# Operands of an RWKV-7 scan prepared in another order: two blocks of items instead of pairs for feature tiles 4 to 7

## The chip, the cores and the metric

The kernel runs on one core of a Trainium2 chip. The metric is device time in microseconds (us) of one execution. TensorE (PE) does the matrix products, VectorE (DVE), ScalarE (ACT) and GpSimd (POOL) the elementwise work, SyncE (SP) issues nearly all transfers between HBM and SBUF, in program order.

## The reference, cut to what matters

The model is a block of depth 2 with a model width of 1024, 512 latent tokens and 256 context tokens. Layer 0 mixes tokens by a bidirectional RWKV-7 recurrence, layer 1 by a Hyena convolution; each mixer stands between two half-step SwiGLU layers. The change lies in layer 0, between its projections and its scan:

```python
k = xk @ w_rkv[1]
w_pre = w0 + einsum(tanh(einsum(xw, w1)), w2)
decay = exp(-exp(-softplus(-w_pre) - 0.5))
a = sigmoid(a0 + einsum(einsum(xa, a1), a2))
kk = heads(k * k_k);  kk = kk / norm(kk)
k_dir = heads(k)[None] * (1 + (ah - 1) * heads(k_a))
ka = kk[None] * ah
S, y = _wkv_scan(S0, _fb(heads(decay)), _fb(k_dir), _both(vh), _both(kk), _fb(ka), _both(rh))
...
y = y + sum(rh * k_bonus * r_k) * vh
g = sigmoid(xg @ g1) @ g2
```

The scan runs over all 768 tokens in both directions (d = 0 and 1). Only latent tokens have outputs, so `r` is needed for the 512 latent tokens alone.

## The kernel before

All activations lie with features on the 128 partitions: eight feature tiles m = 0..7, tokens along the free axis. Each fp32 product is a sum of three products of high and low parts (`hh`, `hl`, `lo`; PE lines L481 to L483).

**Projections.** `rwkv_proj` computes the tokens' projections one after the other: k, r, v and, last, the gate's first factor g1, whose results are called `ev` and stored to the scratch tensors `S_h0` and `S_h1` (DMA line L950). All its products run on PE without a pause where their operands are there.

**Preparation.** `rwkv_prep` is a generator that `rwkv_proj` steps between its products. It turns k, r and two low-rank factors into the operands of the scan. Its unit of work is an item: one feature tile m and one half of the tokens, W = 384 columns. Half 0 is tokens 0 to 383, all latent (`wl` = 384). Half 1 is tokens 384 to 767, of which 128 are latent (`wl` = 128). An item passes through three stages, and at each step the `back` of item i-2, the `middle` of item i-1 and the `front` of item i are interleaved:

- `front`: loads k and r (SP), normalizes (PE L993, DVE L995), and for each direction makes decay and a from two low-rank products (PE L1006 with the high part `l2h`, L1007 with the low part `l2l`; ACT L1009).
- `middle`: for each direction DVE L1029 to L1054, ACT L1030 to L1039, and the product of r with the key, L1049 (outputs `rb` and `r`), on POOL, but on DVE for the last two items (`NVEC` = 2, L1025). It writes the operands `AR` to `S_A[g, d, half]` (L1058) and `KD` to `S_K[g, d, half]` (L1063, L1065), where g is 0 for m < 4 and 1 for m >= 4.
- `back`: one small product (PE L1075), a copy (ACT L1078) and the store to `S_b` (SP L1079).

`lora2(m)` brings the second low-rank factor of tile m: a DMA of 256 KB into `l2r`, an ACT cast into `l2h` (L975), a POOL subtraction into `l2l` (L976). All three have a single buffer, so the next tile's factor can be split only when the last product of the item before has read the old one.

**Scan.** `rwkv_scan` walks blocks of two 64-token chunks for each direction; for each block and g, `load` zeroes half of a tile `AG` (ACT L1140 in the first four pairs) and loads the rest from `S_A` (SP L1143) and `KK` from `S_K` (L1147). The first four blocks read only half 1; the first reader of half 0 is the ninth pair. Then come the scores (PE L1211), copies of them (ACT L1219, L1187), triangular selection (POOL L1188), `lanes` (ACT L1235) and the block's inversion on DVE, which begins with the transpose L1240. From the third pair on, a small POOL memset (L1136) of `AG` stands ahead of its load. `selg` (POOL L1566) multiplies two constants for the scan's output; it waits for four small loads `ysum` (SP L1565).

The order of the first stretch of the scan on PE, DVE and POOL is written out by hand; in the preparation, and on ACT and SP everywhere, a list scheduler orders the instructions when the program is built, so a change in one place can swap neighbours elsewhere.

Of the kernel before, what the change touches and what calls it, by code (L numbers as in the profile page):

```python
# [20 lines left out]
DT = D // P  # L21
# [5 lines left out]
NP = 4  # L27
# [249 lines left out]
class K:  # L277
# [678 lines left out]
    def rwkv_prep(self, bp):  # L956
# [5 lines left out]
        l2 = {}  # L962

        def ps(w):
            return self.psq.tile([P, 512], F32, tag="pq", name=self.nm("pq"))[:, :w]

        def T(tag, w=W, bufs=2):
            return bp.tile([P, W], F32, tag=tag, name=self.nm(tag), bufs=bufs)[:, :w]

        def lora2(m):  # L970
            raw = bp.tile([P, 4, P], F32, tag="l2r", name=self.nm("l2r"), bufs=1)
            hi = bp.tile([P, 4, P], F32R, tag="l2h", name=self.nm("l2h"), bufs=1)
            lo = bp.tile([P, 4, P], F32R, tag="l2l", name=self.nm("l2l"), bufs=1)
            nc.sync.dma_start(raw, self.A["wa2"][m])
            nc.scalar.copy(hi, raw)  # L975
            nc.gpsimd.tensor_tensor(lo, raw, hi.bitcast(F32), ALU.subtract)  # L976
            l2[m] = (hi, lo)

        lora2(0)

        def front(s):
            m, half = s["m"], s["half"]
            mc = slice(m, m + 1)
            o = s["o"] = half * W
            wl = s["wl"] = min(TL - o, W)
            s["nl"] = wl // 64
            k, r = T("k"), T("r", wl)
            nc.sync.dma_start(k, self.S_k[m][:, o : o + W])
            nc.sync.dma_start(r, self.S_r[m][:, o : o + wl])
            hi, lo = l2[m]  # L990
            yield
            pb = ps(W)
            nc.tensor.matmul(pb, self.selT[:, m * P : (m + 1) * P], self.kinv[:, o : o + W], start=True, stop=True)  # L993
            kk = s["kk"] = T("kk")
            nc.vector.scalar_tensor_tensor(kk, k, self.hkk[:, mc], pb, ALU.mult, ALU.mult)  # L995
            s["k"], s["r"] = k, r
            yield
            s["q"], s["a"] = [], []
            for d in range(2):
                q = bp.tile([P, nch, 65], F32, tag=f"q{d}", name=self.nm("q"))  # L1000
                a = T(f"a{d}")
                nc.gpsimd.memset(q[:, :, 0:1], 0.0)
                rows = slice(d * 64, d * 64 + 64)
                for j, (x, t) in enumerate(((self.midw, q[:, :, 1:]), (self.mida, a))):
                    pt = ps(W)
                    nc.tensor.matmul(pt, hi[:, 2 * j + d], x[d][:, o : o + W], start=True, stop=False)  # L1006
                    nc.tensor.matmul(pt, lo[rows, 2 * j + d], x[d][rows, o : o + W], start=False, stop=True)  # L1007
                    b = (self.hw0, self.ha0)[j][:, d, mc]
                    nc.scalar.activation(t, c3(pt) if j == 0 else pt, AF.Tanh, bias=b, scale=0.5)  # L1009
                nc.vector.tensor_scalar(q[:, :, 1:], q[:, :, 1:], 1.0, None, ALU.add)  # L1010
                s["q"].append(q)
                s["a"].append(a)
                if d == 1 and half == 0 and m < DT - 1:
                    lora2(m + 1)
                yield

        def middle(s):
# [50 lines left out]
        def back(s):  # L1068
            m, wl, o = s["m"], s["wl"], s["o"]
            pt = ps(wl)  # L1070
            rks = bp.tile([P, P], F32, tag="rks", name=self.nm("rks"), bufs=1)
            nc.scalar.activation(rks, self.c("bo64"), AF.Copy, scale=self.rk32[:, m : m + 1])
            yield
            for d in range(2):
                nc.tensor.matmul(pt, rks, s["b"][d], start=d == 0, stop=d == 1)  # L1075
            yield
            v = s["b"][0]
            nc.scalar.copy(v, pt)  # L1078
            nc.sync.dma_start(self.S_b[s["m"]][:, o : o + wl], v)  # L1079
            yield  # L1080

        items = [dict(i=2 * m + 1 - half, m=m, half=half) for m in range(DT) for half in (1, 0)]
        n = len(items)
        for i in range(n + 2):
            gens = []
            if 0 <= i - 2:
                gens.append(back(items[i - 2]))
            if 0 <= i - 1 < n:
                gens.append(middle(items[i - 1]))
            if i < n:  # L1090
                gens.append(front(items[i]))
            while gens:
                gens = [x for x in gens if next(x, 0) is None]
                yield
# [1030 lines left out]
```

## Time and profile before

| | us |
|---|---|
| median of 3 runs | 3029.62 |
| lowest to highest | 3029.31 to 3033.85 |
| the profiled execution, its own time | 3036.99 |
| its span from first to last instruction | 3035.0 |

| engine | busy us in the span | share |
|---|---|---|
| PE | 2782.4 | 92% |
| DVE | 1818.3 | 60% |
| ACT | 1163.4 | 38% |
| POOL | 477.7 | 16% |

PE bounds the program as a whole. The change lies in the stretch from about 900 to 1010 us after the span's start and touches what follows it, where the shares differ from these, so the rows below are of that stretch. The mean granted clock of PE over the span is 0.947.

### The profile page before, as it was taken

The page shows a single profiled execution, that of the slowest core. Times are in us where ns is not written, and L with a number is a line of the kernel's source. Part 1 is how long each engine was busy: PE and PEld are TensorE (multiplying, and loading weights), DVE is VectorE, ACT ScalarE, POOL GpSimd, SP SyncE. Part 2 cuts the span into 40 slices and gives each one's busy share as a digit, 9 for nine tenths or more (in the row PEclk, how much of TensorE's full clock was granted, in tenths as well). Part 3 has the DMA queues.
Part 4 walks back from the last instruction along what each step waited for, and adds up shares of the span by engine and source line. Part 5 has one row for each costly group of instructions (what it writes and reads, how often), then busy time and mean ns, then how long its engine had stood idle before and what let it go on. Part 6 is the DMA issues. An engine that isn't in the chain of part 4 may idle for free.

```text
span 3035.0 us, 46673 instructions
## 1 busy us (share of the span) xinstructions
PE 2782.4 (92%) x18394; PEld 2324.9 (77%) x18394; DVE 1818.3 (60%) x3403; ACT 1163.4 (38%) x2007; POOL 477.7 (16%) x647
## 2 busy tenths in 40 slices
PE   8899999978889378887899999999999989899998
PEld 4788888857666366765788889888887777888888
DVE  4656444474798688997655546455365588653334
ACT  3221121255666678874232223322334322332222
POOL 0000000032343445532100000000000054100000
PEclk9999999979989678998899999999999999999999
DMA  5434333313688744434345543455333544232331
GB/s 206 155 106 148 132 128 109 100 37 102 171 211 209 192 117 130 125 86 125 128 146 167 171 162 112 140 183 180 106 116 135 206 143 147 105 124 85 97 106 48
DMA packets 363971, 409.36 MB, mean 135 GB/s; under 512 B 77719, under 2 KB 303127, under 8 KB 362024
## 3 DMA queue, kind: packets, MB, share of 16 engines
q1 hardware_dynamic: 363752, 406.39, 42.4%
q8 instruction: 144, 2.36, 0.3%
q14 instruction: 75, 0.61, 0.1%
HBM read 340.20 MB, written 65.34 MB: 134 GB/s over the span
## 4 chain that ended last, share of the span: by engine, by line
PE 74%; DVE 13%; DMA 4%; ACT 3%; issue 3%; POOL 2%; SPq 0%; DVEq 0%; POOLq 0%; ACTq 0%
PE ps L481 21%; PE ps L482 21%; PE ps L483 21%; DVE Dl L1278 1%; PE sc L1211 1%; DVE wlo L487 1%; DVE Tm L1271 1%; DMA mraw<-in_mod_wt 1%; DVE SV L1350 1%; DVE zt L1946 1%; POOL za L1947 1%; DVE zl L487 1%; PE pf L1759 1%; DMA AG<-S_A 1%; DMA x<-in_xT 1%
## 5 line engine op out<-in xcount | busy, mean ns | idle before, releaser
L482 PE MATMUL ps<-hl,whi 128*128 128x512 f32 (+1 forms) x2064 | 742.4, 362 | 3.5 <-DVE hl L268 3.5
L481 PE MATMUL ps<-hh,whi 128*128 128x512 f32 (+1 forms) x2064 | 732.2, 363 | 14.2 <-ACT hh L267 10.7
L483 PE MATMUL ps<-hh,wlo 128*128 128x512 f32 (+1 forms) x2064 | 735.6, 362 | 2.0 <-DVE wlo L487 2.0
L487 DVE TENSOR_TENSOR wlo<-raw,whi 128x1024 fp32r<-128x1024 f32 (+1 forms) x325 | 392.9, 1215 | 383.6 <-ACT whi L486 382.6
L486 ACT CAST whi<-raw 128x1024 fp32r<-128x1024 f32 (+1 forms) x338 | 344.6, 1028 | 707.8 <-PE ps L482 631.2
L481 PEld LDWEIGHTS ps<-hh,whi 128*128 128x128 f32 x2064 | 386.7, 190 | 78.3 <-ACT hh L267 13.2
L482 PEld LDWEIGHTS ps<-hl,whi 128*128 128x128 f32 x2064 | 392.8, 190 | 64.4 <-DVE hl L268 4.9
L483 PEld LDWEIGHTS ps<-hh,wlo 128*128 128x128 f32 x2064 | 391.8, 190 | 63.4 <-DVE wlo L487 2.9
L481 PE MATMUL ps<-dh,whi 128*128 128x512 f32 (+1 forms) x1072 | 354.3, 336 | 7.8 <-DVE x L660 7.8
L482 PE MATMUL ps<-dl,whi 128*128 128x512 f32 (+1 forms) x1072 | 358.3, 335 | 0.0
L483 PE MATMUL ps<-dh,wlo 128*128 128x512 f32 (+1 forms) x1072 | 357.8, 335 | 0.0
L421 DVE CUSTOM_DVE_ANT_0 mraw<-mraw,mc 128x1024 f32<-128x1024 f32 x128 | 156.5, 1223 | 142.8 <-DMA mraw<-in_mod_wt 141.6
L481 PEld LDWEIGHTS ps<-dh,whi 128*128 128x128 f32 x1072 | 203.5, 190 | 29.4 <-DVE x L660 8.0
L482 PEld LDWEIGHTS ps<-dl,whi 128*128 128x128 f32 x1072 | 204.2, 190 | 20.5
L483 PEld LDWEIGHTS ps<-dh,wlo 128*128 128x128 f32 x1072 | 204.0, 190 | 20.2
L375 POOL COPY mraw<-dl 128x1 f32<-128x1 f32 x128 | 44.8, 364 | 896.3 <-DVE dl L487 631.2
L611 DVE TENSOR_TENSOR sg<-sg,ps 128x512 f32<-128x512 f32 (+1 forms) x110 | 69.1, 633 | 175.6 <-PE ps L483 165.5
L610 ACT ACTIVATE sg<-ps 128x512 f32<-128x512 f32 (+1 forms) x110 | 59.8, 553 | 209.7 <-PE ps L483 202.8
L486 ACT CAST dh<-sg 128x512 fp32r<-128x512 f32 (+1 forms) x110 | 62.1, 575 | 201.2 <-DVE sg L611 201.1
L482 PE MATMUL ps<-xl,whi 128*128 128x512 f32 (+2 forms) x336 | 125.8, 376 | 9.6 <-DVE xl L811 7.1
L481 PE MATMUL ps<-xh,whi 128*128 128x512 f32 (+2 forms) x336 | 123.6, 380 | 9.5 <-issue 5.9
L483 PE MATMUL ps<-xh,wlo 128*128 128x512 f32 (+2 forms) x336 | 123.2, 372 | 0.0
(315 smaller groups left out, 4498.6 us busy)
## 6 DMA issues: line engine op xcount, KB each, us to landing
raw<-in_wgu SPq DMA_DIRECT2D x88, 1024.0 KB, 5.0
mraw<-in_mod_wt SPq DMA_DIRECT2D x128, 512.0 KB, 5.3
raw<-in_wd SPq DMA_DIRECT2D x24, 1024.0 KB, 5.0
raw<-in_wrkv SPq DMA_DIRECT2D x12, 1024.0 KB, 5.9
S_A<-AR SPq DMA_DIRECT2D x32, 384.0 KB, 3.6
AG<-S_A SPq DMA_DIRECT2D x48, 256.0 KB, 4.2
KK<-S_K SPq DMA_DIRECT2D x24, 512.0 KB, 4.5
KL<-S_K SPq DMA_DIRECT2D x48, 256.0 KB, 2.9
```

The source lines that it names most:

```text
L375: self.nc.gpsimd.tensor_copy(raw[:, :1], held)
L421: nc.vector.tensor_tensor_reduce(dst, raw, self.rows[w], 1.0, 0.0, ALU.mult, ALU.add, accum_out=cols[w][:, m : m + 1])
L481: nc.tensor.matmul(out, wh, xh, start=start, stop=False)
L482: nc.tensor.matmul(out, wh, xl, start=False, stop=False)
L483: nc.tensor.matmul(out, wl, xh, start=False, stop=stop)
L486: self.nc.scalar.copy(hi, src)
L487: (self.nc.gpsimd if pool else self.nc.vector).tensor_tensor(lo, src, hi.bitcast(F32), ALU.subtract)
L610: nc.scalar.activation(sg, pg, AF.Silu)
L611: nc.vector.tensor_mul(sg, sg, pu)
L1211: nc.tensor.matmul(sc[:, p_, :, :ns, :], KK[:, c, p_].rearrange("p s t -> p (s t)"), AG[:, c, :, p_, :ns, :], start=True, stop=True,)
L1271: nc.vector.tensor_tensor(tm[:, js, rs], L[:, p, rs].unsqueeze(1).to_broadcast([P, n, w]), Dl[:, js, p : p + 1].to_broadcast([P, n, w]), A ...
L1278: nc.vector.tensor_tensor(Dl[:, js, rs], Dl[:, js, rs], tm[:, js, rs], ALU.subtract)
```

## The change

The sixteen items stay, their work is the same, and tiles 0 to 3 keep their order (half 1, then half 0 of each). For tiles 4 to 7 the order was 4/1, 4/0, 5/1, 5/0, 6/1, 6/0, 7/1, 7/0 (tile/half); it is now 4/1, 5/1, 6/1, 7/1, 4/0, 5/0, 6/0, 7/0. So the tile differs between neighbours in all of these items, and `lora2` is called whenever the next item has another tile: 12 calls in all instead of 8. The last two items, whose L1049 products run on DVE, are now both of half 0 (384 wide); before, they were one of each half.

```diff
-            l2[m] = (hi, lo)
-
-        lora2(0)
+            l2["next"] = (hi, lo)
...
-            hi, lo = l2[m]
+            hi, lo = l2.pop("next")
...
-                if d == 1 and half == 0 and m < DT - 1:
-                    lora2(m + 1)
+                if d == 1 and s["i"] < n - 1:
+                    if items[s["i"] + 1]["m"] != m:
+                        lora2(items[s["i"] + 1]["m"])
+                    else:
+                        l2["next"] = (hi, lo)
...
-        items = [dict(i=2 * m + 1 - half, m=m, half=half) for m in range(DT) for half in (1, 0)]
+
+        order = [(m, half) for m in range(NP) for half in (1, 0)] + [(m, half) for half in (1, 0) for m in range(NP, DT)]
+        items = [dict(i=i, m=m, half=half) for i, (m, half) in enumerate(order)]
         n = len(items)
+        lora2(0)
```

The line numbers of the changed kernel differ by -2 to +4 from those named above (L1211 is L1215 there, L1143 is L1147, L1566 is L1570, L1075 is L1076).

Where instructions stand, three places. The first is SP's queue where the preparation ends and the scan's first loads begin. `S_h` are the stores of the gate's first factor, `AG` and `KK` the scan's loads. Before:

```order
362 L950 DMA S_h1_4898<-ev_1348_8230 32x512
363 L1058 DMA S_A111_4908<-AR_1345_8193 128x6x128
364 L1065 DMA S_K111_4916<-KD_1346_8197 64x6x64
365 L1063 DMA S_K111_4916<-KD_1346_8197 64x6x128
366 L1065 DMA S_K111_4916<-KD_1346_8197 64x6x64
367 L1143 DMA AG_1362_8322<-S_A001_4902 64x2x512
368 L1058 DMA S_A100_4905<-AR_1353_8250 128x6x128
369 L1065 DMA S_K100_4913<-KD_1355_8255 64x6x64
370 L1143 DMA AG_1362_8322<-S_A001_4902 64x2x512
371 L1147 DMA KK_1363_8323<-S_K001_4910 128x2x512
```

And now, from the same store of `S_h1` on:

```order
368 L950 DMA S_h1_4898<-ev_1360_8254 32x512
369 L1566 DMA selg_8341<-in_selq 128x256
370 L1569 DMA ysum_8340<-in_lng 32x256
371 L1066 DMA S_K100_4913<-KD_1367_8279 64x6x64
372 L1569 DMA ysum_8340<-in_lng 32x256
373 L1059 DMA S_A100_4905<-AR_1365_8274 128x6x128
374 L1064 DMA S_K100_4913<-KD_1367_8279 64x6x128
375 L1066 DMA S_K100_4913<-KD_1367_8279 64x6x64
376 L1147 DMA AG_1374_8346<-S_A001_4902 64x2x512 x2
377 L1151 DMA KK_1375_8347<-S_K001_4910 128x2x512
382 L1569 DMA ysum_8340<-in_lng 32x256
386 L1569 DMA ysum_8340<-in_lng 32x256
```

Seven transfers stand between the store of `S_h1` and the first load of the scan, where four stood; the four small loads for `selg`, which stood ahead of the `S_h` stores, are spread out, the last one ten places behind the first `AG` load.

The second place is POOL at the same point of the program, before (`AG_1370` is the second block's first tile):

```order
194 L487 TENSOR_TENSOR xl_1290_7984<-xm_1288_7980,xh_1289_7983 128x512
195 L1566 TENSOR_TENSOR selg_8317<-selg_8317,ysum_8316 128x256
196 L1188 AFFINE_SELECT AG_1362_8322<-AG_1362_8322 64x4x64 x4
197 L1188 AFFINE_SELECT AG_1364_8329<-AG_1364_8329 64x4x64 x2
198 L1136 MEMSET AG_1370_8372 128x4
```

and now (`AG_1382` is the second block's first tile):

```order
195 L976 TENSOR_TENSOR l2l_1325_8088<-l2r_1323_8086,l2h_1324_8087 128x512
196 L487 TENSOR_TENSOR xl_1299_8004<-xm_1297_8000,xh_1298_8003 128x512
197 L1050 TENSOR_TENSOR rb_1313_8053<-r_1252_7823,a0_1259_7845 128x384
198 L1050 TENSOR_TENSOR r_1252_7823<-r_1252_7823,a1_1264_7864 128x384
199 L1192 AFFINE_SELECT AG_1374_8346<-AG_1374_8346 64x4x64 x4
200 L1192 AFFINE_SELECT AG_1376_8353<-AG_1376_8353 64x4x64
201 L1570 TENSOR_TENSOR selg_8341<-selg_8341,ysum_8340 128x256
202 L1192 AFFINE_SELECT AG_1376_8353<-AG_1376_8353 64x4x64
203 L1140 MEMSET AG_1382_8396 128x4
```

`selg` went from ahead of the selections to between them, ahead of the memset of the second block's tile; and a split of the low-rank factor (`l2l`) now stands ahead of the last `xl` of the projections.

The third place is PE from the end of the projections to the scan's first scores, before:

```order
4449 L482 MATMUL ps_1347_8205<-xl_1290_7984,whi_1328_8112 32x512
4450 L483 MATMUL ps_1347_8205<-xh_1289_7983,wlo_1329_8113 32x512
4451 L1075 MATMUL pq_1349_8234<-rb_1333_8150,rks_1350_8235 128x128
4452 L1075 MATMUL pq_1349_8234<-r_1299_8014,rks_1350_8235 128x128
4453 L1211 MATMUL ps_1367_8339<-AG_1362_8322,KK_1363_8323 128x128 x4
4454 L1211 MATMUL ps_1368_8350<-AG_1362_8322,KK_1363_8323 128x128 x4
4455 L1075 MATMUL pq_1360_8282<-rb_1354_8253,rks_1361_8283 128x384
```

and now:

```order
4437 L482 MATMUL ps_1359_8229<-xl_1299_8004,whi_1340_8138 32x512
4438 L483 MATMUL ps_1359_8229<-xh_1298_8003,wlo_1341_8139 32x512
4439 L1076 MATMUL pq_1330_8112<-rb_1313_8053,rks_1331_8113 128x384
4440 L991 MATMUL pq_1336_8130<-kinv_807_5887,selT_4942 128x384
4441 L1004 MATMUL pq_1348_8181<-mw0_4938,l2h_1324_8087 128x384
4450 L1076 MATMUL pq_1361_8258<-rb_1345_8176,rks_1362_8259 128x384
4451 L1076 MATMUL pq_1361_8258<-r_1308_8034,rks_1362_8259 128x384
4452 L1215 MATMUL ps_1379_8363<-AG_1374_8346,KK_1375_8347 128x128 x4
4455 L1215 MATMUL ps_1384_8404<-AG_1376_8353,KK_1377_8354 128x128 x4
4456 L1076 MATMUL pq_1372_8306<-rb_1366_8277,rks_1373_8307 128x384
```

The last item's low-rank products moved from ahead of the last projection products to behind them, and the last item's two `back` products from between the first scores to behind all four groups of the first block.

## Rows read from the trace of the kernel before

**Rows 1.** Busy time by stretch: PE, PEld, DVE, ACT, POOL; granted clock; DMA share; GB/s.

```profile
900.00:940.00 40.00, 38.50 (x183) 28.82 (x182) 34.84 (x53) 27.92 (x61) 14.67 (x16) 0.96 0.96 243
980.00:990.00 10.00, 6.91 (x19) 3.33 (x18) 10.00 (x21) 7.04 (x14) 1.73 (x3) 0.83 0.74 169
990.00:1000.00 10.00, 0.79 (x2) 0.50 (x2) 5.69 (x13) 7.27 (x12) 3.49 (x1) 0.53 0.96 243
...
1060.00:1380.00 320.00, 265.08 (x4539) 219.75 (x4538) 280.77 (x849) 244.78 (x539) 144.19 (x228) 0.88 0.40 112
```

**Rows 2.** Timeline of PE: start, us, line, out<-in, [idle before <-releaser].

```profile
986.08 0.39 PE L483 MATMUL ps<-xh,wlo 128*32 128x512 f32 x1
...
1004.08 3.76 PE L1211 MATMUL ps<-AG,KK 128*128 128x128 f32 x16 [11.73 <-DMA AG<-S_A]
1007.63 0.88 PE L1075 MATMUL pq<-rb,rks 128*128 128x384 f32 x2
...
1008.99 1.05 PE L1211 MATMUL sc<-AG,KK 128*128 128x128 f32 x8
```

**Rows 3.** Timeline of SP's transfers: time of issue, time the issue took, line.

```profile
989.92 0.63 SPq L950 DMA_DIRECT2D S_h<-ev  x1
...
994.03 0.60 SPq L1143 DMA_DIRECT2D AG<-S_A  x1
...
996.93 0.61 SPq L1147 DMA_DIRECT2D KK<-S_K  x1
...
1009.69 0.33 SPq L1079 DMA_DIRECT2D S_b<-rb  x1
...
1012.07 1.25 SPq L1143 DMA_DIRECT2D AG<-S_A  x2
```

**Rows 4.** Timeline of ACT at the start of the scan.

```profile
993.58 3.20 ACT L1140 ACTIVATE AG<-ones 64x1024 f32<-64x1024 f32 x3 [2.09 <-POOL selg L1566]
...
1009.19 0.48 ACT L1078 COPY rb<-pq 128x384 f32<-128x384 f32 x1
...
1011.37 0.62 ACT L486 CAST gh<-gr 128x512 fp32r<-128x512 f32 x1
...
1013.33 2.13 ACT L1140 ACTIVATE AG<-ones 64x1024 f32<-64x1024 f32 x2
1015.37 2.48 ACT L1235 COPY Dl<-Bc 32x512 f32<-32x512 f32 x4
```

**Rows 5.** Timeline of DVE, end of the preparation and first two inversions.

```profile
965.71 1.45 DVE L1010 TENSOR_SCALAR q<-q 128x384 f32<-128x384 f32 x1
...
973.25 0.34 DVE L1010 TENSOR_SCALAR q<-q 128x384 f32<-128x384 f32 x1
...
986.95 0.28 DVE L1049 TENSOR_TENSOR rb<-r,a 128x128 f32<-128x128 f32 x1
...
1004.91 0.56 DVE L1049 TENSOR_TENSOR rb<-r,a 128x384 f32<-128x384 f32 x1 [2.57 <-DMA S_b<-rb]
...
1017.94 1.93 DVE L1240 STREAM_TRANSPOSE L<-Dl 128x1024 f32<-128x1024 f32 x1 [11.81 <-ACT Dl L1235]
...
1034.90 1.91 DVE L1240 STREAM_TRANSPOSE L<-Dl 128x1024 f32<-128x1024 f32 x1 [0.24 <-ACT Dl L1235]
```

**Rows 6.** POOL's group of the factor splits, 780 to 1005 us: busy us, mean ns.

```profile
L976 POOL TENSOR_TENSOR l2l<-l2r,l2h 128x512 fp32r<-128x512 f32 x7 | 11.8, 1687 | 3.1 <-ACT l2h L975 3.0
```

**Rows 7.** Timeline of POOL at two places.

```profile
965.34 1.61 POOL L976 TENSOR_TENSOR l2l<-l2r,l2h 128x512 fp32r<-128x512 f32 x1
...
989.67 3.82 POOL L1566 TENSOR_TENSOR selg<-selg,ysum 128x256 f32<-128x256 f32 x1 [6.93 <-DMA ysum<-in_lng]
...
1011.95 0.10 POOL L1136 MEMSET AG<- 128x4 f32 x1
```

**Rows 8.** What PE waited for, 780 to 986 us: total, times, longest.

```profile
PE pq L1007 <- POOL l2l L976: 0.6, 1, 0.6
```

**Rows 9.** Transfers by kind, 780 to 1005 us: KB each, median us to landing.

```profile
ysum<-in_lng SPq DMA_DIRECT2D x4, 32.0 KB, 2.2
```

## The prediction

> **What bounds the kernel now.** I read the busy time by stretch first. From 900 to 940 us PE is busy for 38.50 of 40 us: the projections run there, and the preparation only fills the other engines. From 980 to 990 us DVE is busy for 10.00 of 10 us and PE for 6.91; the tail of the preparation hangs on DVE. From 990 to 1000 us nothing is full except the transfers, at a share of 0.96: PE works 0.79 us and DVE 5.69 [rows 1]. That is the seam between preparation and scan, and it is the only place where the order of items could give something large. In PE's timeline the last projection product starts at 986.08 and the first scores at 1004.08, after 11.73 us of idle time that a load of `AG` ended [rows 2].
>
> The next question is what holds that load back, because the change pays only if it is the data of half 1. SP's timeline answers it. The store of `S_h1` is issued at 989.92, the first `AG` load at 994.03, `KK` at 996.93 [rows 3]. ACT zeroes the tiles of these loads at 993.58, 2.09 us after it was free [rows 4]; the row blames `selg`, but `selg` ends at 993.49 by its own row [rows 7], and the zeroed tiles lie in the memory that the projections gave back, so I take the end of the last projection's results (`ev`, `S_h`) to be what is waited for too. The half-1 data of tile 7 come from the item before the last, whose stores stand directly ahead of that load in SP's queue (first order listing). So half 1 is late by little or nothing; the memory opens at the same time.
>
> Then DVE. It idles 11.81 us until the transpose of the first block's inversion at 1017.94, and the second block's transpose at 1034.90 waits only 0.24 us [rows 5]. The second block's tile is loaded at 1012.07 [rows 3], right behind the POOL memset at 1011.95 [rows 7]. From 1060 to 1380 us DVE is busy for 280.77 of 320 us and PE for 265.08 [rows 1], so what DVE loses at the start of the scan is hardly made up later.
>
> **The change part by part.** The sum is made against the profiled execution, 3036.99 us, which lies 7.37 us above the median of the runs, 3029.62; the difference found is put on the median. A difference of 0.2%, 6.06 us, is about what a measurement of this kernel can tell from no change.
>
> *Four more factor loads.* Each adds a transfer of 256 KB, an ACT cast and a POOL split. The seven splits in the rows took 11.8 us, 1.69 us each [rows 6]. POOL is busy for 14.67 of 40 us from 900 to 940 us [rows 1], so 4 x 1.69 = 6.8 us find room. What hides them from PE are the projection products that stand between the last low-rank product of an item and the first of the next, 26 to 34 PE rows in the new order. In the rows before, PE waited for the split once, 0.6 us, in seven reloads [rows 8]. With that share four more cost 0.3 us; if each waited as long as the one did, 2.4 us; if none did, 0. I take +0.3. The transfers are 4 x 256 KB = 1.05 MB at 243 GB/s, 4.3 us of transfer time in a stretch whose share is already 0.96 [rows 1]. They are prefetched a whole item ahead into `l2r`, so nothing waits for them unless the k and r loads behind them do; I take 0, and keep +4.3 as the upper bound.
>
> *A split beside DVE.* While the split at 965.34 ran on POOL, DVE's L1010 took 1.45 us instead of 0.34 [rows 5, 7]. So each further split in the stretch where DVE is full costs DVE up to 1.1 us. One of the four falls there (the last, which stands ahead of the last `xl`): +1.1, bounds 0 and 2.2 (two of them). The Trainium skill, page SBUF — State Buffer, section "SBUF: two separate sides", says that VectorE and GpSimd take a shared pair of ports as an exclusive lock, and that the loser waits for the whole instruction. By it the loss would be up to the split's whole 1.6 us instead of 1.1; the row agrees in kind, since L1010 ended just after the split did.
>
> *A heavier end.* Items 14 and 15 are now both 384 wide in r. DVE's `rb` and `r` products of item 14 grow from 0.28 to 0.56 us each [rows 5], and the two L1047 by about as much: 4 x 0.28 = +1.1 us on DVE at the end. Against it, PE does the last projection products ahead of the last item's low-rank products instead of behind them (third listing), so `S_h1` can be stored 1 to 2 us earlier. With the split that is +1.1 +1.1 -1.9 = +0.3 for the store of `S_h1`, bounds -2 and +3.
>
> *SP's queue.* Behind that store seven transfers instead of four stand ahead of the first `AG` load, but the two `AG` loads now stand together and `KK` directly behind. An issue takes about 0.6 us [rows 3]. Seven issues are 4.3 us, against 4.1 before (989.92 to 994.03); `KK`, which completes the first scores' operands, comes two issues after that plus 0.6: about 990.2 + 4.3 + 1.2 + 0.6 = 996.3 to 997.5, against 996.93. I take +0.5 for the first scores, with the bounds -2 and +3 of the store.
>
> *First block.* ACT's `lanes` no longer stand behind the copy `rb` (0.48), the cast `gh` (0.62) and two zeroings (2.13): 3.2 us earlier [rows 4]. The last scores no longer stand behind the `back` products: 1008.99 - 1007.63 = 1.4 us earlier [rows 2]. So DVE starts the first inversion up to 4 us earlier. I cost this at nothing, since what is late next is the second block: its transpose, which DVE meets in a hand-written order in the middle of the first inversion, had only 0.24 us of slack [rows 5], and DVE would wait there for what it saved.
>
> *selg.* It now stands on POOL ahead of the memset that opens the second block's load (second listing). In the row it took 3.82 us while DVE was full [rows 7]. By its size, half of a split, it would be 0.84 us. At the new place DVE is idle, so I take it nearer to the latter: +1.0, bounds 0.8 and 3.8. Everything of the second block moves by the first scores' shift plus this: +1.5.
>
> *The rest.* Behind the scan the scheduler swaps a few neighbours on ACT, SP and PE; I cost that at 0, with 2 us either way, by the size of the waits that I saw there.
>
> The sum is 0.3 (PE waiting for splits) + 0.5 (first scores) + 1.0 (`selg`) = +1.8 us; with the part of the reloads' other bounds that is likelier up than down I put it at +2: 3039.0 in the profiled execution's terms, 3031.6 us as a median. The bounds: -2 + 0.8 - 2 = -3 at the low end, and 2.4 + 3 + 3.8 + 2 = +11 at the high end, if all fell together.
>
> **The rivals.**
>
> *A: slower, through selg.* The last of the four `ysum` loads stands ten places behind the first `AG` load on SP, behind a store to `S_b` that waits for item 14's `back` product. In the rows the last such store was issued at 1009.69 [rows 3]. If the new one is issued as late, the load follows at about 1011, lands 2.2 us later [rows 9], and `selg` takes 3.8: 1017.0 before the memset, instead of 1011.95. That is +5.1 for the second block, and the third term of the sum is 5.1 in place of 1.5; with +0.3 and SP's queue behind it (`KK` of the second block stands behind the same store) it is +6 to +9, 3036 to 3039 us. It decides from an issue of that load at about 1012. Against it: in the rows item 14's `back` is on PE long before the scores (third listing, and ahead of them still), so its store should come some 10 us earlier. Chance 0.26.
>
> *B: faster, because half 1 was what the scan waited for.* If the zeroing of the first tiles and the first loads are held by tile 7's stores and not by memory, the loads can now start when the projections end: at about 988 instead of 994.03, 6 us earlier, and with the 3.2 us of the `lanes` the first two blocks come 6 to 9 us earlier; 3020.6 to 3023.6 us. It decides from a first `AG` load at 990 or before. Against it: seven transfers, one of them `S_K` of half 0, are written ahead of that load in SP's new queue. Chance 0.13.
>
> *C: the change does not do what it says.* The early half 1 helps nobody, because the order in which the queues and the memory open is as before. This is my forecast's own case; it includes all outcomes within 6 us. Chance 0.61.
>
> **How the numbers follow.** The likeliest is C with +2: 3031.6 us; its own range is 3026 to 3036. To hold 8 in 10 I reach into A up to 3039 and into B down to 3023.5, which leaves about 1 in 10 on either side. Faster by over 0.2% has 0.13 (B), slower by over 0.2% has 0.26 (A), the rest is 0.61.
>
> **What the profile after would show.** Right: first scores at 1003 to 1006 us; a first `AG` load within 2 us of 994; the first transpose earlier than the first scores' shift says, and then a wait of DVE ahead of the second transpose; `selg` between the selections and under 1.5 us long; PE waiting for splits under 1 us in all. Wrong: the last `ysum` load issued after 1008 (rival A); a first `AG` load before 990 (rival B); PE's projections ending over 2 us later than 986.08, which would mean that the reloads or the 1.05 MB of transfers are not hidden; or a stretch behind 1060 us that differs by more than the start of the scan does.

## The result, and the profile after

The changed kernel takes 3047.55 us in the median of 8 runs (3038.87 to 3055.57); the kernel before takes 3029.93 us in 8 runs. The ratio is 1.0053, with a 95% interval of 1.0034 to 1.0072: slower by about 16 us. A second set of 6 runs (below) gives 1.0058. The profiled execution has a span of 3040.3 us, only 5.3 us above that of before; that one execution of before lay 7 us above its median and that of the changed kernel (3042.36) 5 us below its own, so the two spans understate the difference, and the losses are read from stretches and not from the ends. From the last product of the scan's output projection to the end of the span, where nothing was changed, that execution of before took 1530.7 us, and those of all the other runs 1521.8 to 1526.4. From the last product of the SwiGLU layer ahead of the projections to the last product of the output projection it was 888.1 us before and is 902.6 now.

The stretches of the changed kernel, in the columns of [rows 1]:

```profile
940.00:980.00 40.00, 33.60 (x133) 21.16 (x132) 34.05 (x51) 25.30 (x55) 18.69 (x15) 0.87 0.84 218
980.00:990.00 10.00, 6.83 (x18) 2.83 (x18) 10.00 (x17) 5.28 (x13) 4.23 (x3) 0.93 0.54 124
990.00:1000.00 10.00, 4.19 (x7) 1.73 (x6) 7.30 (x14) 7.99 (x12) 0.00 (x0) 0.50 0.91 219
...
1060.00:1380.00 320.00, 267.13 (x4525) 220.28 (x4520) 280.90 (x838) 243.70 (x536) 143.23 (x228) 0.87 0.38 111
```

The scan itself, from 1060 to 1380 us, reads as in [rows 1]. From 940 to 980 us PE is busy for 33.60 of 40 us at a granted clock of 0.87; the kernel before was bound by PE there, at 1.00:

```profile
940.00:980.00 40.00, 38.98 (x179) 26.37 (x178) 36.44 (x56) 26.81 (x60) 16.72 (x22) 1.00 0.78 190
```

PE's waits from 940 to 986 us (total, times, longest) name what it lacked in the changed kernel:

```profile
PE pq L1004 <- DVE kk L993: 3.6, 1, 3.6
PE ps L482 <- POOL q L1000: 1.8, 1, 1.8
PE ps L482 <- POOL xl L487: 1.1, 1, 1.1
PE ps L481 <- ACT xh L486: 0.9, 1, 0.9
```

None of them is a wait for a split of the factor. PE waits for the projections' own operands `xl` and `xh` and for `kk` (the wait put down to `q` ends with the `xl` just ahead of it on POOL). In the same stretch of the kernel before, PE waits once:

```profile
PE pq L1075 <- POOL r L1049: 1.0, 1, 1.0
```

POOL's timeline shows where `xl` stands:

```profile
969.24 5.03 POOL L487 TENSOR_TENSOR xl<-xm,xh 128x512 fp32r<-128x512 f32 x1 [2.55 <-ACT xh L486]
974.21 0.10 POOL L1000 MEMSET q<- 128x6 f32 x1
978.42 1.29 POOL L976 TENSOR_TENSOR l2l<-l2r,l2h 128x512 fp32r<-128x512 f32 x1 [4.10 <-ACT l2h L975]
980.31 1.75 POOL L487 TENSOR_TENSOR xl<-xm,xh 128x512 fp32r<-128x512 f32 x1 [0.60 <-ACT xh L486]
982.02 1.32 POOL L1050 TENSOR_TENSOR rb<-r,a 128x384 f32<-128x384 f32 x1
983.42 1.19 POOL L1050 TENSOR_TENSOR r<-r,a 128x384 f32<-128x384 f32 x1
...
1012.23 0.72 POOL L1570 TENSOR_TENSOR selg<-selg,ysum 128x256 f32<-128x256 f32 x1
```

POOL idles 4.10 us for the cast `l2h`, splits the factor at 978.42, and then come the last `xl`, `rb` and `r`, in one row until 984.6. The split itself does not hold up that `xl`, which waits 0.60 us more for its operand `xh`; `xh` stands on ACT behind the cast of the factor. The cast had waited for PE, because its buffer was still being read. ACT's timeline:

```profile
977.61 0.62 ACT L975 CAST l2h<-l2r 128x512 fp32r<-128x512 f32 x1 [2.12 <-PE pq L1004]
...
979.62 0.60 ACT L486 CAST xh<-xm 128x512 fp32r<-128x512 f32 x1
...
983.79 0.53 ACT L1037 ACTIVATE Ep<-q 128x390 f32<-128x390 f32 x1 [2.90 <-DVE KD L1055]
985.07 0.71 ACT L1031 ACTIVATE a<-a,omka,hka 128x384 f32<-128x384 f32 x1 [0.74 <-DVE ka L1030]
...
986.10 0.57 ACT L841 ACTIVATE ev<-ps 128x512 f32<-128x512 f32 x1
...
994.86 2.12 ACT L1144 ACTIVATE AG<-ones 64x1024 f32<-64x1024 f32 x2 [1.08 <-DMA S_h<-ev]
```

DVE's timeline, beside that row on POOL and at the first two inversions:

```profile
970.45 0.55 DVE L1055 TENSOR_TENSOR KD<-a,q 128x384 f32<-128x384 f32 x1
...
980.93 1.55 DVE L1054 TENSOR_TENSOR KD<-ka,Ep 128x384 f32<-128x384 f32 x1
982.40 1.36 DVE L1055 TENSOR_TENSOR KD<-a,Ep 128x384 f32<-128x384 f32 x1
983.68 1.35 DVE L1030 SCALAR_TENSOR_TENSOR ka<-a,kk 128x384 f32<-128x384 f32 x1
...
988.63 0.41 DVE L949 TENSOR_SCALAR ev<-ev 32x512 f32<-32x512 f32 x1
...
1016.64 1.93 DVE L1244 STREAM_TRANSPOSE L<-Dl 128x1024 f32<-128x1024 f32 x1 [5.40 <-ACT Dl L1239]
...
1036.56 1.91 DVE L1244 STREAM_TRANSPOSE L<-Dl 128x1024 f32<-128x1024 f32 x1 [3.89 <-ACT Dl L1239]
```

Three DVE instructions of 0.55 us take 1.35 to 1.55 us each while POOL works, 2.6 us in all. ACT waits for them, and `ev`, the projections' last result, stands behind on ACT. PE and SP:

```profile
982.11 0.51 PE L482 MATMUL ps<-xl,whi 128*128 128x512 f32 x1 [1.11 <-POOL xl L487]
...
982.91 0.40 PE L483 MATMUL ps<-xh,wlo 128*32 128x512 f32 x1
...
991.77 1.34 SPq L950 DMA_DIRECT2D S_h<-ev  x1
...
997.41 1.69 SPq L1147 DMA_DIRECT2D AG<-S_A  x2
...
1006.09 3.45 PE L1215 MATMUL ps<-AG,KK 128*128 128x128 f32 x16 [7.01 <-DMA S_A<-AR]
...
1013.43 1.25 SPq L1147 DMA_DIRECT2D AG<-S_A  x2
```

The last product ends at 983.3 (982.91 + 0.40), `ev` begins at 986.10, and the last `S_h` store is issued at 991.77, 8.5 us after the last product; before it was 989.92 - 986.47 = 3.4 us [rows 2, 3]. Of the 5.0 us more, 3.0 pass until DVE has finished `ev` (989.04, 5.7 us after the last product; 2.8 before), and 2.0 on SP, where a store of `S_b` and two of `S_K` are issued ahead of this one (2.7 us from `ev` to the store; 0.7 before). The landing of that store opens the zeroing at 994.86, then come the loads and the scores. From the end of the last product to the first scores it is 22.8 us now and was 17.6; this stretch is called the seam below.

The second place is the end of the scan, of which no rows were shown. The kernel before, ACT (1432, 1434 us), SP (1429, 1434 us) and PE (1433 us):

```profile
1432.20 0.77 ACT L1374 ACTIVATE SV<-pss 64x256 f32<-64x256 f32 x2
...
1434.23 1.99 ACT L486 CAST whi<-raw 128x1024 fp32r<-128x1024 f32 x2 [1.26 <-DMA raw<-in_wo]
...
1429.12 1.34 SPq L460 DMA_DIRECT2D raw<-in_wo  x2
...
1434.39 0.37 SPq L1454 DMA_DIRECT2D pv<-S_v  x1
...
1433.02 0.69 PE L1382 MATMUL pss<-SV,KT 128*64 128x64 f32 x16 [1.64 <-ACT SV L1374]
```

And the changed kernel, ACT, SP and PE:

```profile
1439.51 1.99 ACT L486 CAST whi<-raw 128x1024 fp32r<-128x1024 f32 x2 [2.04 <-DMA raw<-in_wo]
1441.41 0.76 ACT L1378 ACTIVATE SV<-pss 64x256 f32<-64x256 f32 x2
...
1434.44 8.91 SPq L460 DMA_DIRECT2D raw<-in_wo  x3
...
1445.03 0.37 SPq L1458 DMA_DIRECT2D pv<-S_v  x1
...
1442.23 1.12 PE L1386 MATMUL pss<-SV,KT 128*64 128x64 f32 x16 [5.54 <-ACT SV L1378]
```

The last copy of the scan's solution (`SV`) now stands on ACT behind two casts of the output projection's weights, which wait for their load; PE's last step of the scan waits 5.54 us for it instead of 1.64. On SP three weight loads stand in a row instead of two; the third waits for a free buffer, and `pv`, which the scan's post-processing needs, is issued at 1445.03 behind it, 10.6 us later than before; counted from the last inversion's transpose it is 6.5 us. From the last inversion's transpose to the output projection's first product it is 79.3 us (1385.38 to 1464.66), and was 72.4 (1381.28 to 1453.66). PE's clock follows. From 1440 to 1460 us, before and after:

```profile
1440.00:1460.00 20.00, 13.97 (x106) 9.76 (x106) 17.00 (x45) 2.31 (x4) 8.90 (x8) 0.71 0.96 289
```

```profile
1440.00:1460.00 20.00, 9.36 (x70) 4.58 (x71) 15.15 (x26) 7.41 (x10) 6.42 (x6) 0.50 0.94 256
```

PE, with more waits, works there at the lower of its two levels throughout (0.50 of 2.4 GHz).

### The profile page after: what moved, and what is told of

It reads as the page before. It is cut to its first block, busy times and chain, and to the rows that moved or that the text cites. A ratio compares the mean times of both kernels' runs of the same rounds, so it can differ in the third digit from the quotient of the medians.

```text
span 3040.3 us, 46670 instructions
## 1 busy us (share of the span) xinstructions
PE 2785.8 (92%) x18394; PEld 2323.9 (76%) x18394; DVE 1822.7 (60%) x3403; ACT 1165.2 (38%) x2011; POOL 481.1 (16%) x651
## 4 chain that ended last, share of the span: by engine, by line
PE 45%; DVE 4%; issue 1%; DMA 1%; POOL 1%; ACT 0%; DVEq 0%; ACTq 0%; POOLq 0%; SPq 0%
PE ps L482 14%; PE ps L483 14%; PE ps L481 14%; DVE wlo L487 1%; PE pf L1763 1%; DVE zt L1950 1%; POOL za L1951 1%; PE pf L481 0%; PE pf L483 0%; DVE zl L487 0%; PE pf L482 0%; DVE za L1947 0%; DVE nx L254 0%; DVE gv L1972 0%; DVE hl L268 0%
```

## The experiments

Ratios are against the kernel before, run beside each on the same chip, with 95% intervals. old_order_reload, dma_only, work_apart and dve_split ran on another chip than the other experiments.

| run | median us | ratio | interval |
|---|---|---|---|
| changed kernel | 3047.55 | 1.0053 | 1.0034 to 1.0072 |
| again | 3050.02 | 1.0058 | 1.0040 to 1.0076 |
| out_order_back | 3043.04 | 1.0038 | 1.0024 to 1.0053 |
| out_order_back_2 | 3042.18 | 1.0033 | 1.0021 to 1.0046 |
| before_out_order | 3033.09 | 1.0007 | 0.9996 to 1.0017 |
| before_out_order_2 | 3035.43 | 1.0009 | 1.0000 to 1.0019 |
| no_reload | 3030.65 | 1.0001 | 0.9991 to 1.0012 |
| old_order_reload | 3037.89 | 1.0026 | 1.0012 to 1.0040 |
| dma_only | 3033.34 | 1.0012 | 0.9999 to 1.0025 |
| work_apart | 3034.01 | 1.0018 | 1.0007 to 1.0029 |
| work_apart_2 | 3033.76 | 0.9999 | 0.9989 to 1.0009 |
| chain_only | 3034.73 | 1.0004 | 0.9993 to 1.0015 |
| chain_work | 3036.85 | 1.0016 | 1.0004 to 1.0028 |
| dve_split | 3038.07 | 1.0033 | 1.0019 to 1.0047 |
| two_buffers | 3029.88 | 0.9989 | 0.9978 to 1.0000 |
| before_two_buffers | 3039.48 | 1.0021 | 1.0009 to 1.0034 |

**again.** 

> The changed kernel once more, with a second profile. In its first profiled execution it lost against the one before in two places: about 8 us of PE time at the seam between preparation and scan (960 to 1005 us), and 7 us at the scan's end (1440 to 1480 us), where the clock was low for 19.1 us instead of 11.5; and it won about 6 us behind 2500 us, where the clock was low for less time. Theory (two places, both set by the order of instructions): the ratio is 1.004 to 1.007 again, the two losses stand in the second profile too, and what differs between executions is the time at the low clock. Rival (the result was a matter of the executions): the ratio falls under 1.002.

Ratio 1.0058. From the last product to the first scores it is 22.6 us, from the last transpose to the output projection 79.5 us: both losses stand again. The 19.1 us of low clock in the expectation do not come out of the first profile: from 1440 to 1480 us the granted clock was 0.63 there and 0.86 before, which is about 30 and 11 us at the lower level.

**out_order_back and its repetition.** The two casts, the third weight load and the third pair of casts are queued behind what they had overtaken:

```diff
+            pins = {0: self.last_sv, 1: last_x, 2: self.last_sq}
...
+        def fetch(p):
+            with self.tc.issue_after(pins[p].ins) if p in pins else ExitStack():
+                return self.wload()
```

> The changed kernel, with the instructions at the scan's end held in the order that they have in the kernel before: on ACT the weight casts for the output projection behind the last copy of the solution, on SP the third weight load behind the loads of the post-processing. The preparation is as in the changed kernel. Theory (the scan's end costs about 7 us, and more when the clock stays low for longer): 6 to 12 us under the changed kernel, 3036 to 3042 us, and in the profile the last copy of the solution waits for no weight load. Rival (all of the loss comes from the seam and is carried through): within 2 us of the changed kernel.

> The changed kernel with the scan's end held as before once more, for the interval and a second profile. Theory: 1.003 to 1.0045, below the changed kernel's 1.0053 and 1.0058. Rival (the scan's end is no cost of its own): 1.005 or more.

ACT and SP of the first of these runs:

```profile
1437.70 0.77 ACT L1382 ACTIVATE SV<-pss 64x256 f32<-64x256 f32 x2
1439.71 1.99 ACT L486 CAST whi<-raw 128x1024 fp32r<-128x1024 f32 x2 [1.24 <-DMA raw<-in_wo]
...
1442.54 0.37 SPq L1462 DMA_DIRECT2D pv<-S_v  x1
```

The copy no longer stands behind the casts, and the stretch to the output projection is 73.2 us (73.8 in the repetition). The ratio falls by 0.15 to 0.25%, 5 to 8 us: less than the whole loss. Taken one by one the intervals overlap; both pairs together give 0.20%, 6 us, with an interval of about 1 to 11 us. The seam is unchanged: 22.3 and 23.0 us from the last product to the first scores.

**before_out_order and its repetition.** The reverse edit, on the kernel before: the same three things are forced ahead.

> The kernel before, with the scan's end put into the order that the changed kernel has there; the preparation is untouched. Theory: 6 to 12 us slower than before, ratio 1.002 to 1.004, with PE's last step of the scan waiting about 4 us longer for ACT and the post-processing's loads about 8 us later. Rival (the order there is hidden, or is only a result of the seam): within 2 us of before.

> The kernel before with the scan's end in the changed kernel's order once more: its first interval, 0.9996 to 1.0017, left open whether it costs anything by itself. In its profile the stretch from the last inversion's transpose to the end of the output projection took 127.7 us, and 122.8 in the kernel before. Theory: 1.0008 to 1.0020. Rival (it costs only behind a late scan): under 1.0005.

PE's last step waits 5.54 and 5.63 us for the copy here too, and the stretch grows from 72.4 to 76.0 and 77.9 us. The ratio rises by 0.07 and 0.09%, about 2.5 us: less than the first expectation, in the range of the second, and the two intervals together are only just above nothing. The order at the scan's end brings that wait by itself; whether it costs more behind the changed preparation (6 us against 2.5) these intervals do not tell.

**no_reload.** The four extra reloads are left out, and the order of items stays.

```diff
-                    if items[s["i"] + 1]["m"] != m:
+                    if items[s["i"] + 1]["m"] != m and s["i"] < 11:
```

> The changed order of items with the scan's end held as before, and without the four extra reloads' work: the last four items use the low-rank factor of tile 7 instead of their own, so their decay and a are not those of the reference; 8 loads, casts and splits in all, as before. Theory (the seam's loss comes from the reloads, whose splits hold POOL and DVE and delay the last projection products): 3029 to 3033 us, equal to before within 3 us, with PE's last projection product at about 980 us. Rival (the loss comes from the order itself, four wide items at the end): as the run with the reloads and the same scan's end, 3036 to 3042 us.

1.0001, with an interval of 0.1% either way: no cost and no gain of the order of items by itself can be seen. ACT, SP and PE of this run:

```profile
979.91 0.59 ACT L845 ACTIVATE ev<-ps 32x512 f32<-32x512 f32 x1 [0.26 <-PE ps L483]
...
983.96 1.11 SPq L954 DMA_DIRECT2D S_h<-ev  x1
...
997.04 3.75 PE L1219 MATMUL ps<-AG,KK 128*128 128x128 f32 x16 [7.73 <-DMA AG<-S_A]
```

`ev` follows the last product directly (its end is at 979.87), the store is issued 4.1 us behind it instead of 8.5, and the first scores come after 17.2 us instead of 22.8. From the last product of the SwiGLU layer to the last of the output projection it took 888.1 us, as in the kernel before; with the reloads (out_order_back, both times) 897.2 and 897.7. But PE's waits do not all go with the reloads: in the 48 us ahead of the end of the last product they add up to 4.9 us here, to 8.3 and 8.2 us with the reloads, and to 1.0 us before. The wait for `kk` (about 3 us) is gone, waits for `xl` and `xh` stay.

**old_order_reload.** The kernel before, with a reload between the two halves of tiles 4 to 7.

```diff
+                if d == 1 and half == 1 and m >= NP:
+                    lora2(m)
```

> The kernel before, with its order of items and its order at the scan's end, but with the factor of tiles 4 to 7 loaded, cast and split again between the two halves of each: the four extra reloads alone. Theory (the reloads are the seam's loss, in whatever order the items come): 3037 to 3044 us, ratio 1.002 to 1.005. Rival (they cost only together with four wide items at the end): 3029 to 3033 us.

The scan's end is held in the order of the kernel before, as in no_reload. 1.0026: the reloads cost in the old order too. From the last product to the first scores it is 23.4 us. Here `ev` follows the last product at once, but a like row stands one step later, on POOL and ACT:

```profile
989.86 1.71 POOL L980 TENSOR_TENSOR l2l<-l2r,l2h 128x512 fp32r<-128x512 f32 x1 [4.24 <-ACT l2h L979]
...
994.55 0.71 ACT L1036 ACTIVATE a<-a,omka,hka 128x384 f32<-128x384 f32 x1 [2.49 <-DVE ka L1035]
```

`rb` and `r` follow the split on POOL, three DVE instructions beside them take 1.13 to 1.35 us, ACT waits for the last of these, and behind it the zeroing of `AG` begins 12.3 us after the last product instead of 7.1.

**dma_only, work_apart, chain_only, chain_work, dve_split.** These take the reload apart. In dma_only the four transfers stay and nothing else; work_apart adds cast and split in place in the raw tile; chain_only has no transfer, and a cast and a split of one column of each block in the factor in use; chain_work does the same with all columns; dve_split is the whole reload with the split on DVE.

```diff
+        def spare(hi, lo):
+            nc.scalar.copy(hi[:, :, 0:1], hi[:, :, 0:1].bitcast(F32))
+            nc.gpsimd.tensor_tensor(lo[:, :, 0:1], lo[:, :, 0:1].bitcast(F32), hi[:, :, 0:1].bitcast(F32), ALU.subtract)
```

(chain_only; the others differ in these lines alone, and dve_split passes DVE to `lora2`.)

> The changed order, the scan's end held as before, and of the four extra reloads only the four transfers of 256 KB; no cast and no split, and the last four items use the factor of tile 7, so their decay and a are not those of the reference. Theory (the transfers are hidden; what costs is the split on POOL beside DVE and the wait for the single buffer): as without reloads, 3029 to 3033 us. Rival (1.05 MB more in a full stretch holds up the k and r loads): 3036 to 3043 us, most of the reloads' cost.

> As the run with the four transfers alone, but with the four casts on ACT and the four splits on POOL too, done in place in the raw tile, so that no product waits for them and they wait for no product; the last four items use the factor of tile 7. It parts the work from the chain. Theory (the splits' place on POOL, which pushes the projections' own splits and the r products on POOL into the stretch where DVE is full): 3035 to 3041 us, more than half of the 12 us that the reloads cost. Rival (the chain through the single buffer, last product, cast, split, next product): 3029 to 3033 us, as without reloads.

> The changed kernel with the scan's end held as before, and the four extra splits on DVE instead of POOL; it computes all of the reference. Theory (POOL's place is what costs): 4 to 9 us under the run with the splits on POOL, 3034 to 3039 us, with the last evacuation of the projections within 1 us of the last product instead of 2.5 us behind it. Rival (the chain through the single buffer): within 2 us of that run, 3041 to 3045 us.

> The changed order, the scan's end held as before, and of the extra reloads only the chain through the single buffer: no transfer, and a cast and a split of one column of each block (4 of 512 columns) written into the factor in use, so that they wait for the last product of one item and the next item's products wait for them; the last four items use the factor of tile 7. Theory after the last four runs (the chain is the larger part of the reloads' 11 us: 1.0038 with all of it, 1.0018 with the work apart from it): 1.0015 to 1.0025, 3034 to 3037 us, and last low-rank products 4 us or more behind the projections' last. Rival (only transfers, casts and splits cost): under 1.0008.

> The run with the work apart from the chain once more, for the interval. Theory: 1.0005 to 1.0020, under the chain's and clearly under the whole reloads'. Rival (it is the work): 1.003 or more.

> The changed order with the scan's end held as before; of the four extra reloads the full cast and the full split (512 columns each), written into the factor in use, so that they stand in the chain between the last product of one item and the next item's products; no transfer. The last four items use the factor of tile 7. Theory now (it takes the chain and the full work together, since only then do the split, and the splits and products queued behind it on POOL, come late): 1.0025 to 1.004, as the whole reloads. Rival (the transfers are the part that was missing): under 1.0015.

The theory that POOL's place alone costs fell with dve_split (1.0033, as with POOL). Its profile did what that theory asked: `ev` follows the last products at once, the store is issued 4.1 us after the last one ends, and the first scores come after 18.6 us. The loss stayed, so the row from the split through DVE and `ev` to the store cannot be the whole of the reloads' cost. dma_only is the reverse case: a seam of 23.4 us, and 1.0012. The theory that the chain alone costs fell with chain_only (1.0004). The work apart from the chain gave 1.0018 and 0.9999, no clear cost; the transfers 1.0012, with an interval that touches nothing. The chain with the full work gave 1.0016, about half of the whole reloads, between what the theory and its rival had said. No part has the cost of the whole; the transfers' 0.12% and the 0.16% of the chain with the full work add up to 0.28%, so the parts may simply add, and nothing here shows that they must act together.

**two_buffers and before_two_buffers.** All reloads stay, but the factor has two buffers. The low part keeps only the half that is read, and the raw tile comes in two pieces, so that it fits. This recuts the work as well: the split is four POOL instructions of 64x128 (0.66 us each in the median) instead of one of 128x512 (1.56 us), the cast is two of 128x256. The scan's end is held in the order of before in both runs.

```diff
-            raw = bp.tile([P, 4, P], F32, tag="l2r", name=self.nm("l2r"), bufs=1)
-            hi = bp.tile([P, 4, P], F32R, tag="l2h", name=self.nm("l2h"), bufs=1)
-            lo = bp.tile([P, 4, P], F32R, tag="l2l", name=self.nm("l2l"), bufs=1)
+            hi = bp.tile([P, 4, P], F32R, tag="l2h", name=self.nm("l2h"), bufs=2)
+            lo = bp.tile([P, 2, P], F32R, tag="l2l", name=self.nm("l2l"), bufs=2)
+            for j in range(2):
+                raw = bp.tile([P, 2, P], F32, tag="l2r", name=self.nm("l2r"), bufs=1)
...
+                    nc.gpsimd.tensor_tensor(lo[r, j], raw[r, d], hi[r, 2 * j + d].bitcast(F32), ALU.subtract)
```

> The changed kernel with the scan's end held as before, all reloads kept, and the chain broken: the factor's high and low part have two buffers each, which fits because the low part keeps only the half that is read and the raw tile is loaded in two pieces of 128 KB. All of the reference is computed. Theory (without the chain the reloads' work is hidden): 1.000 to 1.0015. Rival (the work itself, or the smaller pieces, cost as much): 1.003 or more.

> The kernel before with the same two buffers for the factor; its order and its eight reloads stay. Theory (its three reloads between tiles 4 to 7 stand where the projections' products cover them): within 0.1% of before. Rival (the chain costs there as well): 0.998 to 0.999, which would be a version faster than both.

With two buffers and the scan's end held, the changed order takes 0.9989 of before, instead of 1.0033 to 1.0038 with one buffer. By the ratio it is the fastest of all runs here, 3 us under the kernel before, with an interval that ends at 1.0000. In its profile no cast waits for a product any more, only for its transfer. ACT, SP and PE of its profile:

```profile
991.45 1.06 ACT L845 ACTIVATE ev<-ps 128x512 f32<-128x512 f32 x2 [1.29 <-PE ps L483]
...
995.86 0.38 SPq L954 DMA_DIRECT2D S_h<-ev  x1
...
1005.70 1.62 PE L1222 MATMUL ps<-AG,KK 128*128 128x128 f32 x6 [2.87 <-DMA AG<-S_A]
```

`ev` follows the products again, the store comes 4.0 us behind the last one (991.88), and the scores 13.8 us behind it. In this execution the products themselves ended later than in the others, and PE's waits in the 48 us ahead of that end were 7.4 us, so this profile does not show where the gain comes from; it is read from the repeated runs alone. The same two buffers on the kernel before make it slower, 1.0021, against both of that run's expectations. Its scan took 355.2 us from the second to the last transpose, 346.4 before, with no wait that I could tie to the edit. I take it that rebuilding the order of instructions can move the time by 0.2% with nothing taken away or added that costs so much; no run tests that. If so, differences of up to 0.2% between two of these programs cannot be put down to their edit, and that holds for every part of the reload taken alone.

## Why the prediction was wrong

The forecast was 3031.6 us, held between 3023.5 and 3039; measured were 3047.55.

**What was right.** `selg` stood between the selections and took 0.72 us, forecast 1.0. The load of the second block moved from 1012.07 to 1013.43, +1.4, forecast +1.5. The first transpose came 1.3 us earlier, and DVE then waited 3.89 us for the second block instead of 0.24 [rows 5]. PE waited for no split. Half 1 was not what the scan waited for: no_reload shows no gain from it. Rival A named the right side and the wrong mechanism: the last `ysum` load was issued before 1008 and `selg` was short.

The first scores were forecast 0.5 us later and came 2.0 later (1006.09). That lies inside the bounds by luck: that execution of the kernel after had reached the end of its products 3.2 us earlier than the one of before. Counted from that end the scores came 5.2 us later and the second transpose 4.8 us. The first `AG` load came at 997.41, outside the 2 us around 994 that the prediction had named.

**The first step that failed** is the price of four more factor loads, "+0.3", with the words that the projection products hide them from PE. As they stand in the change the reloads cost 0.33 to 0.38% once the scan's end is held, 10 to 11 us; without them it is 0.01%. I priced PE's wait for the split, and PE never waited for a split. What I left out is what is queued behind the cast on ACT (the `xh` of the projections and with it `xl`) and behind the split on POOL (`rb` and `r`), and that the cast can't begin before the item's last product has read the buffer. PE's waits from 940 to 986 us went from 1.0 to 7.8 us (the four rows above and 0.4 us for an `xl` on DVE). By no_reload about 3 us of these belong to the reloads; the rest stays without them, and there the time is that of the kernel before.

**The second is a size.** The store of `S_h1` was put at +0.3 us, "bounds -2 and +3", made of a split beside DVE, wider items and earlier products. Against the last product it came 8.5 us later instead of 3.4, +5.0. The products did end ahead of the last item's low-rank products, as said; but `xl`, `rb` and `r` had moved into the stretch where DVE is full, three DVE instructions beside them took 2.6 us more, `ev` stood behind on ACT, and on SP other stores stood ahead of it.

**The third** is "The rest": "I cost that at 0, with 2 us either way". The swap of neighbours at the scan's end, visible in the order of instructions, moved that stretch by 6.9 us; held back, it took 0.15 to 0.25% off the ratio, 5 to 8 us. The prediction had named the sign itself, a stretch behind 1060 us that differs by more than the start of the scan.

Shown: four reloads through the single buffer cost, taken out of the changed order (no_reload) and put into the old one (old_order_reload), and in these two pairs the seam is short without them and long with them (17.2 against 22.3 and 23.0 us, 17.6 against 23.4); the order at the scan's end brings a wait of its own, taken out (out_order_back) and put in (before_out_order), of which the size in the whole time is known only roughly. With two buffers the loss is gone, but that edit changes the split too, so that the single buffer is the cause is likely and not shown. Open: how the reload's cost divides. Chain with small work, work without chain and transfers alone cost 0.00 to 0.18%, chain and full work 0.16%, the whole 0.33 to 0.38%. The row of waits above (product, cast, `xh` and split, `xl`, `rb` and `r`, DVE, `ev`, store) is read from the profile; that it makes the difference is argued, not shown, and dve_split, which lost as much without it, speaks against it as the only cause. Each of these edits also rearranges the program.

## What to carry to other kernels

A reload into a single buffer is not priced by its consumer's wait, which was nothing here. It begins when the last reader ends, and everything queued behind its cast and its split on their engines begins later too; follow each of those queues to the next engine that is full. Where a scheduler orders the program, a change in one place reorders others: look at the order of instructions at every stage's end for loads and casts that now stand ahead of a last result, and price them. Executions of one kernel can differ by as much as the change (17 us here): compare stretches between fixed events, and let repeated runs decide.

## What was not expected of the hardware

POOL instructions of one form, splits of 128x512, took very different times: `l2l` 1.29 us at 978.42, where DVE idled until 978.87, and `xl` 5.03 us at 969.24, while DVE ran without a gap until 973.22. DVE's instructions of 0.55 us took up to 1.55 us beside POOL's later ones. Which of the two engines is held up changes from one instruction to the next, and on POOL it can come to four times the shortest time seen.
